# Weight tiles of sixteen blocks for eight, and more pairs of weight blocks by seven products, in a hybrid decoder layer

## The chip, the cores and the metric

The kernel runs on one core of a Trainium2 chip. The metric is device time in microseconds (us) of one execution. Before the change it is 1799.46 us, the median of three runs from 1799.2 to 1799.68.

## The reference, cut to what matters

One layer of a decoder for 264 tokens (a prompt of 256 and 8 sampled ones), width 2048, inner width of the feed-forward parts 5504. All inputs are float32.

```python
def swiglu(x, wg, wu, wd):
    return (jax.nn.silu(x @ wg) * (x @ wu)) @ wd
...
h = h + 0.5 * swiglu(rmsnorm(h, norm_ffn1), ffn1_gate, ffn1_up, ffn1_down)
mix, ... = mixing_block(rmsnorm(h, norm_mix), w_in, b_gates, conv_w, conv_b, norm_mlstm, norm_conv, w_out, ...)
h = h + mix
h = h + 0.5 * swiglu(rmsnorm(h, norm_ffn2), ffn2_gate, ffn2_up, ffn2_down)
y = rmsnorm(h, norm_final)
```

`mixing_block` is one projection `w_in`, four mLSTM heads beside a short gated convolution, and the projection `w_out`. The change touches how the weights of all these products are brought in and split, and how the products of the two feed-forward parts ("ffn 1", "ffn 2") are made.

## The kernel before

**Blocks and halves.** Activations lie with the width on the partitions: 16 blocks of 128 (`KB`) by 264 tokens. A weight block is 128 x 128. The inner width is 43 blocks, worked in two halves, 0 to 21 and 22 to 42. For each half comes first the gate and up products, one inner block after another (16 weight blocks each for gate and up, `product`, or `product_pair` for both at once), then the down products of that half, 16 output blocks of 22 or 21 weight blocks each, added to `h`. So the program is: ffn 1 with gate/up, down, gate/up, down; the mixing; ffn 2 in the same four stages; the last norm.

**Splitting.** TensorE multiplies in f16. A float32 weight tile `wraw` is split on the chip into a high half, written by ScalarE (`high`, L243), and a low half, written by VectorE from the raw weights and the high half (`low`, L251). Both lie in a tile `w`. A product takes three matmuls for each weight block: high by high, high by low, low by high (`three`, L325 to L327), each of 264 columns.

**Pairs by seven.** Two products over the same activations, gate and up of one inner block or two neighbouring output blocks of down, can be made together as a pair (`product_pair`). The main part, high by high, is ordinary (L390, 264 columns). The two small corrections of every four weight blocks (two of each product) are made with seven products of half the tokens, 132 columns, instead of eight (L374, L375). For that the kernel needs sums of the weight halves (`weight_sums`, four instructions on VectorE for each 2 x 8 weight blocks, L304, into a tile `s`), sums of the activations (`token_sums`, L362, called the forms, made once: for the gate/up products from the norm, for the down products from each eight finished inner blocks, by `act_form`), and afterwards a joining of the PSUM banks (`join`: a copy on ScalarE at L430, then L433 to L440 on VectorE). `GU_SEVEN` lists the inner blocks whose gate and up go by seven, 36 in all, every second one from block 7 of ffn 1, from block 3 of ffn 2, and from block 22 of both; `DOWN_SEVEN` lists 17 of the 32 pairs of output blocks by ffn and half.

**Tiles.** `weight_plan` lists all weight tiles in the order of use: tiles of up to eight blocks (`WK`), so two for a gate, two for an up, three for an output block of down; a pair's tiles alternate between its two rows. `fetch` (L264) takes the next of the plan: a DMA of the SP queue into one of six buffers `wraw`, the high half at once into one of seven buffers `w`, and the low half when `release` is called. With `lag` set the low half of a tile waits in `held` until the next `fetch`. `AHEAD` is how many tiles are on the way before one is used. The first two inner blocks, gate and up, are made together from sixteen small tiles of four weight blocks (`FIRST`, `products4`, L542), while the input and its norm come in.

**Order.** The order on each engine is that in which the program issues its instructions (`manual_schedule`). Work that follows a product is put off with `at(delta, ...)`: `tick` counts 1 at the start of a product and a half within it, and then runs what was put off to that count. So the joining of a pair and the decay of gate and up (`halves`) run one count behind the pair, and the splitting of an activation one count later.

**Another path.** The program also holds a path with float32 matmuls for inputs outside f16's range, taken after a check on the values; `half_size` tells the two apart, and the profiled execution is the f16 one.

## Time and profile before

| | |
|---|---|
| median of three runs | 1799.46 us |
| the profiled execution's own time | 1799.44 us |
| its span | 1797.7 us, granted clock of TensorE 0.998 |
| ScalarE, high halves (L243) | 692 instructions, 667.3 us |
| VectorE, low halves (L251, activations included) | 692 instructions, 800.6 us |
| VectorE, weight sums (L304) | 492 instructions in two groups, 164.6 and 155.8 us |
| DMA | 381.53 MB, mean 212 GB/s; the queue of the weights takes 61.2% of the 16 DMA engines |

The profile counts an engine as busy while an instruction of its kind runs; matmuls are pipelined, so their ends are modelled, and their spacing is read from their starts. In its rows `<-` stands for "written from", a bracket for the idle time before an instruction and what ended it, and a row of the waits reads: engine, what it was to write and its line, what it waited for, total us, times, longest. The stages in order of time: the start to 28 us, gate/up of ffn 1's first half to 239, its down to 353, gate/up of the second half to 572, down to 682; the mixing to 1104; ffn 2's stages to 1335, 1448, 1667 and 1778.

### The profile page before, as it was taken

Reading aid. Unit: us, or ns where it says so; the run is one execution under the profiler, and the core shown is the slowest. Engines: PE = TensorE matmul, PEld = TensorE weight load, DVE = VectorE, ACT = ScalarE, POOL = GpSimd, SP = SyncE. Lnnn points to the kernel's source line nnn. Section 1 sums busy time; section 2 is a strip of 40 time slices with the busy share of each in tenths; the row PEclk is TensorE's granted clock in tenths of the full one; section 3 lists DMA queues with packets and bytes.
Section 4 is the critical chain, followed back from the end, with each engine's and each line's share of the span. In section 5 each row is a group of like instructions: output and inputs, shape, how many; then the busy total and the mean of one; then the engine's idle time right before and its main releaser. Section 6 shows DMA issues by size and latency. Waiting matters only on the chain.

```text
span 1797.7 us, 45488 instructions
## 1 busy us (share of the span) xinstructions
PE 1780.6 (99%) x19080; PEld 1595.9 (89%) x19080; DVE 1565.6 (87%) x2528; ACT 901.8 (50%) x1571; POOL 145.4 (8%) x200
## 2 busy tenths in 40 slices
PE   9999999999999999999999999999999999999997
PEld 8899989999998988888888888899989999999896
DVE  8899979999998898788888866999988999999785
ACT  7544444444445445567566644444444344444443
POOL 0000000000000222222121032000000000000122
PEclk9999999999999999999999999999999999999999
DMA  9667666666666556888887655666666666666653
GB/s 301 205 203 219 190 214 194 198 205 211 202 199 192 184 175 218 291 300 274 282 276 243 223 189 173 204 206 209 197 208 193 205 197 220 200 202 200 192 184 111
DMA packets 118517, 381.53 MB, mean 212 GB/s; under 512 B 14972, under 2 KB 24796, under 8 KB 118304
## 3 DMA queue, kind: packets, MB, share of 16 engines
q1 hardware_dynamic: 109104, 350.53, 61.2%
q0 software_dynamic: 8256, 27.57, 4.5%
q8 instruction: 151, 2.47, 0.6%
q10 hardware_dynamic: 944, 0.45, 0.1%
q14 instruction: 62, 0.51, 0.1%
HBM read 366.72 MB, written 11.78 MB: 211 GB/s over the span
## 4 chain that ended last, share of the span: by engine, by line
PE 92%; DVE 5%; issue 1%; ACT 1%; DMA 0%; SPq 0%; DVEq 0%; ACTq 0%
PE ps L327 20%; PE ps L325 20%; PE ps L326 20%; PE ps L390 11%; PE ps L374 10%; PE ps L375 9%; DVE w L251 2%; DVE s L304 1%; PE ps L542 1%; PE ps L688 0%; PE ps L1393 0%; PE ps L1336 0%; PE ps L1291 0%; ACT w L243 0%; DMA wraw<-in_w1gu 0%
## 5 line engine op out<-in xcount | busy, mean ns | idle before, releaser
L251 DVE SCALAR_TENSOR_TENSOR w<-wraw,w 128x1024 f16<-128x1024 f32 (+3 forms) x692 | 800.6, 1181 | 77.4 <-ACT w L243 76.4
L243 ACT ACTIVATE w<-wraw 128x1024 f16<-128x1024 f32 (+3 forms) x692 | 667.3, 1007 | 169.9 <-issue 75.5
L325 PE MATMUL ps<-x,w 128*128 128x264 f16 x1536 | 423.9, 276 | 0.0
L326 PE MATMUL ps<-x,w 128*128 128x264 f16 x1536 | 423.9, 276 | 0.0
L327 PE MATMUL ps<-x,w 128*128 128x264 f16 x1536 | 423.9, 276 | 0.0
L327 PEld LDWEIGHTS <-w 128*128 128x128 f16 x3372 | 329.9, 98 | 50.1 <-DVE w L251 2.0
L326 PEld LDWEIGHTS <-w 128*128 128x128 f16 x3372 | 329.9, 98 | 49.4
L325 PEld LDWEIGHTS <-w 128*128 128x128 f16 x3372 | 330.2, 98 | 48.2 <-issue 0.6
L325 PE MATMUL ps<-xm,w 128*128 128x264 f16 x896 | 247.3, 276 | 0.0
L327 PE MATMUL ps<-xm,w 128*128 128x264 f16 x896 | 247.3, 276 | 0.0
L326 PE MATMUL ps<-xm,w 128*128 128x264 f16 x896 | 247.3, 276 | 0.0
L390 PEld LDWEIGHTS <-w 128*128 128x128 f16 x1886 | 181.4, 98 | 25.4
L375 PEld LDWEIGHTS <-s 128*128 128x128 f16 x1872 | 181.7, 97 | 0.0
L327 PE MATMUL ps<-a,w 128*128 128x264 f16 (+2 forms) x684 | 180.2, 269 | 1.1 <-DVE w L251 1.1
L374 PEld LDWEIGHTS <-s 128*128 128x128 f16 x1872 | 180.1, 96 | 0.6 <-DVE s L304 0.5
L325 PE MATMUL ps<-a,w 128*128 128x264 f16 (+2 forms) x684 | 180.2, 269 | 0.0
L326 PE MATMUL ps<-a,w 128*128 128x264 f16 (+2 forms) x684 | 180.2, 269 | 0.0
L304 DVE TENSOR_TENSOR s<-s,w 128x1024 f16<-128x1024 f16 (+2 forms) x246 | 164.6, 669 | 4.3
L304 DVE TENSOR_TENSOR s<-w 128x1024 f16<-128x1024 f16 (+2 forms) x246 | 155.8, 674 | 5.3
L390 PE MATMUL ps<-x,w 128*128 128x264 f16 x1152 | 141.3, 276 | 0.0
L375 PEld LDWEIGHTS <-w 128*128 128x128 f16 x1418 | 138.3, 98 | 2.9 <-DVE w L251 0.9
L374 PEld LDWEIGHTS <-w 128*128 128x128 f16 x1418 | 138.1, 97 | 2.0
(273 smaller groups left out, 2295.3 us busy)
## 6 DMA issues: line engine op xcount, KB each, us to landing
wraw<-in_w2gu SPq DMA_DIRECT2D x172, 512.0 KB, 4.6
wraw<-in_w1gu SPq DMA_DIRECT2D x164, 512.0 KB, 4.6
wraw<-in_win SPq DMA_DIRECT2D x112, 512.0 KB, 6.0
wraw<-in_w1d SPq DMA_DIRECT2D x42, 512.0 KB, 4.6
wraw<-in_w2d SPq DMA_DIRECT2D x38, 512.0 KB, 4.4
wraw<-in_w2d SPq DMA_DIRECT2D x42, 448.0 KB, 4.1
wraw<-in_wout SPq DMA_DIRECT2D x32, 512.0 KB, 4.5
wraw<-in_w1d SPq DMA_DIRECT2D x36, 448.0 KB, 4.1
```

Of the source, the lines that this page charges most:

```text
L243: nc.scalar.activation(dst, src, AF.Copy, scale=scale)
L251: nc.vector.scalar_tensor_tensor(dst, src, scale, hi, op0=ALU.mult, op1=ALU.subtract)
L304: nc.vector.tensor_tensor(s[:, out], x, y, op=ALU.add)
L325: nc.tensor.matmul(ps, wh, xk[:, 0, :], start=first, stop=False)
L326: nc.tensor.matmul(ps, wh, xk[:, 1, :], start=False, stop=False)
L327: nc.tensor.matmul(ps, wl, xk[:, 0, :], start=False, stop=last)
L374: nc.tensor.matmul(ps, w[0], x[:, 1], start=first, stop=False)
L375: nc.tensor.matmul(ps, w[1], x[:, 0], start=False, stop=last)
L390: nc.tensor.matmul(ps[:, :T], hi[:, i], xs[i][:, 0], start=(k0 + i == 0), stop=False)
L542: nc.tensor.matmul(ps[j0 + j], w[:, nk * j + k, :], x[k0 + k][:, part, :], start=(k0 + k + n == 0), stop=(k0 + k == KB - 1 and n == 2),)
```

## The change

Five things change together.

1. A weight tile holds sixteen blocks (`WIDE`) instead of eight. Gate, up and each block of the mixing projections are one tile each, an output block of down is two tiles (11 and 11 blocks, or 10 and 11). A pair's two rows lie in one tile, eight blocks of each, so that a gate/up pair is two tiles and a down pair three. There are three buffers of raw weights and four of halves, `AHEAD` is 3, and high and low halves alternate block by block within a tile. One transfer, one high and one low instruction serve a whole tile.
2. The four weight sums take three instructions: the first makes two of them, since b + d and c + d have the same second operand (L339 in the changed kernel), and the other two follow from them (L342, L343).
3. 44 instead of 36 inner blocks go by seven: of every five, the first, third and fourth. 19 instead of 17 output pairs, the two more in the first halves.
4. The small tiles of the start have rings of their own (`small`: eight raw, twelve split) in buffers that the sums and forms use later. The first two output blocks of the mixing are made from tiles that hold both (`products_two`), and the decays of the heads (`bc`) lie in the buffer of the joining.
5. `release` also runs at the start of a product and ahead of a pair's matmuls, and `fetch` in the middle of a product whose weights are one tile. Where two pairs are neighbours, the low half of the first one's activations comes one count earlier (`at(0.5, ...)`).

```diff
+WIDE = 16
...
-    n: [j for half in starts for j in half]
-    for n, starts in (
-        ("1", (range(7, 21, 2), range(22, NFB - 1, 2))), ("2", (range(3, 21, 2), range(22, NFB - 1, 2))),
-    )
+    n: [b0 + i for b0, b1 in ((first, 21), (22, NFB - 1)) for i in range(b1 - b0) if i % 5 in (0, 2, 3)]
+    for n, first in (("1", 7), ("2", 3))
 }
 DOWN_SEVEN = {
-    ("1", 0): (1, 3, 4, 6, 7), ("1", 1): (1, 3, 4, 6),
-    ("2", 0): (1, 3, 4, 6, 7), ("2", 1): (1, 3, 4),
+    ("1", 0): (1, 2, 3, 5, 6, 7), ("1", 1): (1, 3, 4, 6),
+    ("2", 0): (1, 2, 3, 5, 6, 7), ("2", 1): (1, 3, 4),
...
-        parts = -(-n // WK)
+        parts = -(-n // (WIDE if sevens else WK))
...
-    def beside(key, one, other, n):
+    def beside(key, rows, n):
+        rows = rows.rearrange("g p k m -> p g k m")
         for k0 in range(0, n, WK):
-            for w in (one, other):
-                plan.append((key, w[:, k0 : min(k0 + WK, n), :], min(WK, n - k0), 128, 1))
+            n_ = min(WK, n - k0)
+            plan.append((key, rows[:, :, k0 : k0 + n_, :], n_, 128, 2))
...
-                    beside((layer, "gu", j), gu[j, 0], gu[j, 1], KB)
+                    beside((layer, "gu", j), gu[j], KB)
...
-    for k0 in (0, half):
-        for db in range(2):
-            add(("out", db), a["wout"][db][:, k0 : k0 + half], half)
+    if sevens:
+        beside(("two", 0), a["wout"][0:2], KB)
+    else:
+        for k0 in (0, half):
+            for db in range(2):
+                add(("out", db), a["wout"][db][:, k0 : k0 + half], half)
...
-    AHEAD = 6 if half_size else 2
+    AHEAD = 3 if half_size else 2
...
-        raw = wpool.tile([128, WK, 128], F32, tag="wraw", name="wraw", bufs=AHEAD + (not half_size))[:, :n, :m]
-        dst = raw.rearrange("p (f k) m -> p f k m", f=several) if several > 1 else raw
-        nc.sync.dma_start(dst, src)
-        parts = wpool.tile([128, 2, WK, 128], PART, tag="w", name="w", bufs=AHEAD + 1)
-        hi, lo = parts[:, 0], parts[:, 1]
-        pairs = [(raw, (hi, lo), slice(0, m))]
-        if half_size and key == "gates":
-
-            pairs = [(raw[:, :, 32 * g :], (hi, lo), slice(16 * g, 16 * g + 16)) for g in (0, 1)]
+        if half_size and key == "four":
+            raw, parts = small()
+        elif half_size:
+            raw = wpool.tile([128, WIDE, 128], F32, tag="wraw", name="wraw", bufs=3)
+            parts = wpool.tile([128, WIDE, 2, 128], PART, tag="w", name="w", bufs=4)
+            raw = raw[:, :, :m]
...
+        elif several > 1:
+            raw, parts = raw[:, : several * n], parts[:, : several * n]
+            nc.sync.dma_start(raw.rearrange("p (g k) m -> p g k m", g=several), src)
+            pairs = [(raw, parts[:, :, 0], parts[:, :, 1])]
+        else:
+            raw, both = raw[:, :n], parts[:, :n]
+            nc.sync.dma_start(raw, src)
+            pairs = [(raw, both[:, :, 0, :m], both[:, :, 1, :m])]
...
-                beside.append(parts)
-                if len(beside) == 2:
-                    sums.append(weight_sums(*beside, tile_[3] // 2))
-                    beside.clear()
+                sums.append(weight_sums(parts, tile_[3]))
...
-    def weight_sums(one, other, n):
-
-        s = spool[0].tile([128, 4, 2, WK // 2, 128], PART, tag="s", name="s", bufs=3)[:, :, :, :n]
-        a_, b_, c_, d_ = (w[:, :, i : 2 * n : 2] for w in (one, other) for i in (0, 1))
-        for out, x, y in ((0, c_, d_), (1, b_, d_), (2, s[:, 0], b_), (3, s[:, 2], a_)):
-            nc.vector.tensor_tensor(s[:, out], x, y, op=ALU.add)
+    def small():
+        if not rings:
+            raws, parts = [], []
+            for g in range(2):
+                t = spool[0].tile([128, 16 * TH], F32, tag=f"g{g}", name=f"raw{g}")
+                t = t[:, :2048].rearrange("p (i k m) -> p i k m", i=4, k=4)
+                raws += [t[:, i] for i in range(4)]
+            for g in range(3):
+                t = spool[0].tile([128, 4, 4, 2, 128], PART, tag="s", name="part", bufs=3)
+                parts += [t[:, i] for i in range(4)]
+            rings.extend((raws, parts))
+        for r in rings:
+            r.append(r.pop(0))
+        return [r[-1] for r in rings]
+    def weight_sums(w, n):
+        m = n // 2
+        s = spool[0].tile([128, 4, WK // 2, 2, 128], PART, tag="s", name="s", bufs=3)[:, :, :m]
+        a_, b_, d_ = (w[:, i : i + 2 * m - 1 : 2] for i in (0, 1, n + 1))
+        bc = w[:, 1 : 2 * n - 1].rearrange("p (g k) h m -> p g k h m", g=2)[:, :, 0 : 2 * m - 1 : 2]
+        nc.vector.tensor_tensor(
+            s[:, 0:2], bc, d_.unsqueeze(1).to_broadcast([128, 2, m, 2, 128]), op=ALU.add
+        )
+        nc.vector.tensor_tensor(s[:, 2], s[:, 1], b_, op=ALU.add)
+        nc.vector.tensor_tensor(s[:, 3], s[:, 2], a_, op=ALU.add)
...
-    def product(key, x, order, m=128, lead=AHEAD):
+    def product(key, x, order, m=128, soon=False):
         tick()
+        if lag[0]:
+            release()
         ps = bank()[:m, :T]
-        k, half = 0, 0.5
-        while k < len(order):
-            while plan and len(ready) + len(held) < lead:
+        count, k, half = len(order), 0, 0.5
+        while k < count:
+            while plan and len(ready) + len(held) < AHEAD:
                 fetch()
             got, hi, lo, n = ready.pop(0)
             assert got == key, (got, key)
+            one = half_size and n == count
+            if soon and k == 0:
+                fetch()
             for i in range(n):
                 three(
-                    ps, hi[:, i, :m], lo[:, i, :m], x[order[k]], k == 0, k == len(order) - 1
+                    ps, hi[:, i, :m], lo[:, i, :m], x[order[k]], k == 0, k == count - 1
                 )
                 k += 1
-            if lead == AHEAD and (k < len(order) or lag[0]):
+                if one and i == n // 2 - 1 and not soon:
+                    fetch()
+                if one and i == n // 2 - 1:
+                    tick(half)
+            if not one and not soon and (k < count or lag[0]):
                 fetch()
-            tick(half)
-            half = 0
+            if not one:
+                tick(half)
+                half = 0
...
-            tiles = []
-            for _ in range(2):
-                while plan and len(ready) + len(held) < AHEAD or not ready:
-                    fetch()
-                tiles.append(ready.pop(0))
-                assert tiles[-1][0] == key, (tiles[-1][0], key)
-            (_, hi0, lo0, n), (_, hi1, lo1, _) = tiles
+            while plan and len(ready) + len(held) < AHEAD or not ready:
+                fetch()
+            got, hi, lo, n = ready.pop(0)
+            assert got == key, (got, key)
+            release()
             s = sums.pop(0)
+            (hi0, lo0), (hi1, lo1) = ((hi[:, r:], lo[:, r:]) for r in (0, n))
...
-            if k0 < count:
-                fetch()
...
-                    if len(ready) > 2 and more:
+                    if more:
...
-                    at(1.5, low, *rest)
+                    at(0.5 if j in sevens and j + 1 in sevens else 1.5, low, *rest)
...
-                            lead=AHEAD - 3 if final else AHEAD,
+                            soon=final,
...
-            self.bc = mp.tile([128, 2, SEQ], F32, tag="bc", name="bc", bufs=1)
+            if e["half_size"]:
+                bc = tmp.tile([128, 5 * TH], F32, tag="y5", name="bc", bufs=1)
+                self.bc = bc[:, : 2 * SEQ].rearrange("p (j t) -> p j t", j=2)
+            else:
+                self.bc = mp.tile([128, 2, SEQ], F32, tag="bc", name="bc", bufs=1)
```

How this stands on VectorE is shown at three places. The rows are in the order of the program; names carry buffer numbers, L-numbers are those of each kernel. The changed kernel's lines L254, L339 to L343, L411, L479 and L895 are before's L251, L304, L362, L433 and L827.

First, the second half of ffn 1's gate/up, behind the joining of a pair. Before, this is block 24; `w_5872` and `w_5893` are the first two of the four tiles of pair 26, and the ordinary block 25 lies between:

```order
L827 TENSOR_TENSOR y5_5952<-y5_5952,rstd_668 128x528
L251 SCALAR_TENSOR_TENSOR w_5893<-wraw_5891,w_5893 128x1024
L304 TENSOR_TENSOR s_5993<-w_5893 128x1024
L304 TENSOR_TENSOR s_5993<-w_5872,w_5893 128x1024
L304 TENSOR_TENSOR s_5993<-s_5993,w_5872 128x1024 x2
L251 SCALAR_TENSOR_TENSOR w_5990<-wraw_5988,w_5990 128x1024
L846 TENSOR_TENSOR ta_6027<-ps_5963,rstd_668 128x264
```

In the changed kernel this is the joining of block 29, whose neighbour 30 is a pair too; `w_6463` and `w_6554` are the gate and the up tile of the ordinary block 31 behind them:

```order
L895 TENSOR_TENSOR y5_6522<-y5_6522,rstd_621 128x528
L254 SCALAR_TENSOR_TENSOR w_6463<-wraw_6462,w_6463 128x16x128
L863 TENSOR_TENSOR y5_6522<-y5_6522,tb_6524 128x264
L254 SCALAR_TENSOR_TENSOR w_6554<-wraw_6553,w_6554 128x16x128
L254 SCALAR_TENSOR_TENSOR a0_5510<-y5_6522,a0_5510 128x264
L479 TENSOR_TENSOR y5_6693<-y5_6693,ps_6535 128x132
```

Before, the tile behind a joining was the second of the four tiles of a pair that comes after another block; now it is the whole gate tile of the block that comes behind the next pair, and the next joining follows two such tiles.

Second, the forms of the activations. Before (`w_6775` is the last up tile of block 31, `w_6838` the first tile of pair 32):

```order
L251 SCALAR_TENSOR_TENSOR a0_5711<-y5_6596,a0_5711 128x264
L251 SCALAR_TENSOR_TENSOR a0_5711<-tc_6743,a0_5711 128x264
L251 SCALAR_TENSOR_TENSOR w_6775<-wraw_6773,w_6775 128x1024
L362 TENSOR_TENSOR g0_6841<-a0_5711 128x1056 x2
L362 TENSOR_TENSOR g0_6841<-g0_6841,a0_5711 128x1056
L362 TENSOR_TENSOR g0_6841<-a0_5711,g0_6841 128x1056
L251 SCALAR_TENSOR_TENSOR w_6838<-wraw_6836,w_6838 128x1024
L433 TENSOR_TENSOR y5_6923<-y5_6923,ps_6751 128x132
```

In the changed kernel, between the joinings of blocks 37 and 39 (`w_7945` is the second tile of pair 40):

```order
L254 SCALAR_TENSOR_TENSOR a1_6774<-y5_7778,a1_6774 128x264
L254 SCALAR_TENSOR_TENSOR a2_7916<-tc_7913,a2_7916 128x264
L411 TENSOR_TENSOR g1_8006<-a1_6774 128x1056 x2
L411 TENSOR_TENSOR g1_8006<-g1_8006,a1_6774 128x1056
L411 TENSOR_TENSOR g1_8006<-a1_6774,g1_8006 128x1056
L254 SCALAR_TENSOR_TENSOR w_7945<-wraw_7944,w_7945 128x16x128
L339 TENSOR_TENSOR s_8012<-w_7945 128x2048
L342 TENSOR_TENSOR s_8012<-s_8012,w_7945 128x1024
L343 TENSOR_TENSOR s_8012<-s_8012,w_7945 128x1024
L479 TENSOR_TENSOR y5_8092<-y5_8092,ps_7922 128x132
```

The forms are the same four instructions; behind them stood one low half of eight blocks ahead of the next joining, and now stand a whole pair tile's low half and sums.

Third, the end of the first product, where the first ordinary tiles follow the small ones. Before (`w_464` and `w_481` are the last small tiles, `w_498` and `w_503` the first two of the next gate):

```order
L251 SCALAR_TENSOR_TENSOR x11_340<-h12_83,gains_165,x11_340 128x264 x2
L251 SCALAR_TENSOR_TENSOR w_464<-wraw_462,w_464 128x512
L251 SCALAR_TENSOR_TENSOR w_481<-wraw_479,w_481 128x512
L251 SCALAR_TENSOR_TENSOR w_498<-wraw_496,w_498 128x1024
L251 SCALAR_TENSOR_TENSOR w_503<-wraw_501,w_503 128x1024
L752 TENSOR_TENSOR sq0_506<-sq0_506 128x528
```

In the changed kernel (`w_470` and `w_479` are the next gate and up):

```order
L254 SCALAR_TENSOR_TENSOR x11_329<-h12_83,gains_165,x11_329 128x264 x2
L254 SCALAR_TENSOR_TENSOR part_198<-raw1_197,part_198 128x4x128 x2
L254 SCALAR_TENSOR_TENSOR w_470<-wraw_469,w_470 128x16x128
L820 TENSOR_TENSOR sq0_474<-sq0_474 128x528
L254 SCALAR_TENSOR_TENSOR w_479<-wraw_478,w_479 128x16x128
L820 TENSOR_TENSOR sq0_474<-sq0_474 128x528 x2
```

The low half of the first ordinary tile covers sixteen blocks in one instruction where two of eight stood, and the first of the norm's squares (L820) now stands ahead of the up tile.

More of the change, by code (lines that the diff above doesn't have):

```diff
@@ L119, in ffn @@
             for db in range(0, KB, 2):
-                one, other = (d[i][:, b0:b1, :] for i in (db, db + 1))
+                both = d[db : db + 2][:, :, b0:b1, :]
                 if sevens and db // 2 in DOWN_SEVEN[layer, half]:
-                    beside((layer, "dd", half, db), one, other, b1 - b0)
+                    beside((layer, "dd", half, db), both, b1 - b0)
                 else:
-                    add((layer, "d", half, db), one, b1 - b0)
-                    add((layer, "d", half, db + 1), other, b1 - b0)
+                    for i in range(2):
+                        add((layer, "d", half, db + i), both[i], b1 - b0)
     four = a["w1gu"][0:2].rearrange("j g p k m -> p (j g) k m")
@@ L277, in fetch @@
         release()
-        held.append((lows, (key, hi, lo, n), parts))
+        held.append((lows, (key, parts[:, :, 0], parts[:, :, 1], n), parts))
         if not lag[0]:
@@ L290, in release @@
             if tile_[0][1] in ("gu", "dd"):
[L291 to L294 removed]
+                sums.append(weight_sums(parts, tile_[3]))
         held.clear()
[L297 to L304 removed]
+    sums, spool, rings = [], [None], []
+    def small():
[22 more added lines that the diff above has]
+        nc.vector.tensor_tensor(s[:, 3], s[:, 2], a_, op=ALU.add)
         return s
@@ L404, in product_pair @@
                     a_, b_, c_ = (hi0[:, e], lo0[:, e]), (hi0[:, o], lo0[:, o]), (hi1[:, e], lo1[:, e])
-                    w = (a_, b_, c_, *((s[:, f, 0, i], s[:, f, 1, i]) for f in range(4)))[f]
+                    w = (a_, b_, c_, *((s[:, f, i, 0], s[:, f, i, 1]) for f in (1, 0, 2, 3)))[f]
                     ps, rhs, own = (
@@ L450, in product_beside, with products_two @@
         ps = bank()[:, :T]
+        while plan and len(ready) + len(held) < AHEAD:
+            fetch()
+        got, hi, lo, n = ready.pop(0)
+        assert got == key and n == KB, (got, key, n)
+        for k in range(0, n, 4):
+            for term, (w, part) in enumerate(((hi, 0), (hi, 1), (lo, 0))):
+                for c in range(4):
+                    nc.tensor.matmul(
+                        ps[32 * c : 32 * c + 32], w[:, k + c, :32],
+                        x[k + c][:, part, :], start=(k + term == 0),
+                        stop=(k + 4 == KB and term == 2), tile_position=(0, 32 * c),
+                    )
+            if k == KB // 2 - 4:
+                fetch()
+        return ps
+    def products_two(x, order):
+        ps = [bank()[:, :T] for _ in range(2)]
         for k0 in range(0, KB, WK):
+            tick()
             while plan and len(ready) + len(held) < AHEAD:
@@ L454, in product_beside @@
             got, hi, lo, n = ready.pop(0)
-            assert got == key and n == WK, (got, key, n)
-            for k in range(0, n, 4):
-                for term, (w, part) in enumerate(((hi, 0), (hi, 1), (lo, 0))):
-                    for c in range(4):
-                        nc.tensor.matmul(
-                            ps[32 * c : 32 * c + 32], w[:, k + c, :32],
-                            x[k0 + k + c][:, part, :], start=(k0 + k + term == 0),
-                            stop=(k0 + k + 4 == KB and term == 2), tile_position=(0, 32 * c),
-                        )
-            if k0 + n < KB:
-                fetch()
+            assert got == ("two", 0) and n == WK, got
+            for j in range(2):
+                for i in range(n):
+                    k = k0 + i
+                    three(
+                        ps[j], hi[:, WK * j + i], lo[:, WK * j + i], x[order[k]], k == 0,
+                        k == KB - 1,
+                    )
+                if j == 0:
+                    fetch()
+                    tick(0.5)
         return ps
     def products2(keys, x, order):
+        if half_size:
+            return products_two(x, order)
         ps = [bank()[:, :T] for _ in keys]
```

19 lines of the change are left out of this document (15 added, 4 removed).

## The prediction

> **What bounds the kernel now.** I read the page first, then what TensorE (PE) waited for, then both engines in order of time.
>
> ```profile
> PE 1780.6 (99%) x19080; PEld 1595.9 (89%) x19080; DVE 1565.6 (87%) x2528; ACT 901.8 (50%) x1571; POOL 145.4 (8%) x200
> ```
> ```profile
> PE ps L1019 <- DVE ok L1013: 2.3, 1, 2.3
> PE ps L542 <- ACT w L243: 1.3, 2, 0.8
> ```
> PE is the bound: its two longest waits of the whole span are a 2.3 us one in the last microseconds and 1.3 us in the first product. A busy share alone would not prove that the matmuls are dense, so the spacing is read from the order of time:
>
> ```profile
> 82.75 1.96 PE L390 MATMUL ps<-x,w 128*128 128x264 f16 x16
> ...
> 92.79 0.28 PE L325 MATMUL ps<-x,w 128*128 128x264 f16 x1
> ...
> 103.59 0.61 PE L390 MATMUL ps<-x,w 128*128 128x264 f16 x4
> ```
> A gate/up block done by seven ("P") takes 92.79 - 82.75 = 10.04 us, an ordinary block ("N") 103.59 - 92.79 = 10.80 us. So what fewer matmuls save is real time, if their weights are ready.
>
> VectorE (DVE), which makes the low halves and the sums, is nearly full where P and N alternate. Its waits in 353 to 572 us (a second half of gate/up, 219 us) are all of these:
>
> ```profile
> DVE w L251 <- ACT w L243: 6.0, 11, 1.5
> DVE y L433 <- ACT y L430: 2.5, 3, 1.0
> DVE ta L846 <- PE ps L327: 1.6, 1, 1.6
> DVE a L251 <- ACT a L243: 1.1, 2, 0.6
> DVE tc L852 <- PE ps L327: 0.7, 1, 0.7
> ```
> 11.9 us of 219: DVE is occupied 94.6% at one pair in two blocks. The question is whether it can carry three in five.
>
> **The change part by part.**
>
> *Fewer matmul columns.* Eight more gate/up pairs (36 to 44) at 10.80 - 10.04 = 0.76 us: 6.1 us. Two more down pairs (17 to 19), both in first halves. Such a pair lasts 353.23 - 339.42 = 13.81 us:
>
> ```profile
> 339.42 1.96 PE L390 MATMUL ps<-a,w 128*128 128x264 f16 x16
> ...
> 353.23 0.95 PE L390 MATMUL ps<-x,w 128*128 128x264 f16 x7
> ```
> Two ordinary products of 22 blocks are 132 matmuls at 10.80/96 = 0.1125 us, 14.85 us; two pairs save 2.1 us. **PE saves 8.2 us.**
>
> *What DVE pays for a tile.* One period of before, from the joining of a pair's banks (L433) to the next:
>
> ```profile
> 426.33 0.29 DVE L433 TENSOR_TENSOR y<-y,ps 128x132 f32<-128x132 f32 x1 [0.98 <-ACT y L430]
> ...
> 428.98 1.22 DVE L251 SCALAR_TENSOR_TENSOR w<-wraw,w 128x1024 f16<-128x1024 f32 x1
> 430.24 1.29 DVE L304 TENSOR_TENSOR s<-w 128x1024 f16<-128x1024 f16 x2
> 431.45 1.41 DVE L304 TENSOR_TENSOR s<-s,w 128x1024 f16<-128x1024 f16 x2
> 432.78 1.22 DVE L251 SCALAR_TENSOR_TENSOR w<-wraw,w 128x1024 f16<-128x1024 f32 x1
> 433.91 0.43 DVE L846 TENSOR_TENSOR ta<-ps,rstd 128x264 f32<-128x264 f32 x1
> ...
> 442.01 1.22 DVE L251 SCALAR_TENSOR_TENSOR w<-wraw,w 128x1024 f16<-128x1024 f32 x1 [0.46 <-ACT w L243]
> ...
> 444.98 1.32 DVE L362 TENSOR_TENSOR g<-a 128x1056 f16<-128x1056 f16 x2
> ...
> 447.58 1.22 DVE L251 SCALAR_TENSOR_TENSOR w<-wraw,w 128x1024 f16<-128x1024 f32 x1
> 448.72 0.28 DVE L433 TENSOR_TENSOR y<-y,ps 128x132 f32<-128x132 f32 x1
> ```
> Joining: 428.98 - 426.33 = 2.65 us. A low half costs 1.13 (432.78 to 433.91), or 1.26 when the next instruction reads its result (428.98 to 430.24); four sums 2.54 (430.24 to 432.78). So a pair's 16 blocks cost 1.13 + 1.26 + 2.54 = 4.93 us. The forms of the activations (L362) take 2.60 us, once in eight blocks. Without them and the 0.46 wait the period is 448.72 - 426.33 - 0.46 - 2.60 = 19.33; less joining, two pair tiles (9.86) and the four lows of N (4.6) it leaves 2.2 for N's evacuations and the splits of activations.
>
> ```profile
> L251 DVE SCALAR_TENSOR_TENSOR w<-wraw,w 128x1024 f16<-128x1024 f32 x560 | 675.4, 1229 | 65.0 <-ACT w L243 64.4
> ...
> L251 DVE SCALAR_TENSOR_TENSOR w<-wraw,w 128x512 f16<-128x512 f32 x16 | 11.1, 692 | 3.3 <-ACT w L243 2.9
> ```
> From 692 ns for 512 elements and 1229 for 1024 comes 1.05 ns an element; 2048 elements are about 2.2 us, 2.3 with a reader behind. So joining two instructions saves only some 0.07 to 0.15 us. The wide sum of 2048 at 0.53 ns an element (0.605 each in the first two sums) is 1.14, the other two 1.33, and the second of the three now reads what the one just ahead wrote: 2.47 to 2.6. **A wide pair tile costs DVE T = 4.73 (no bubble) to 5.00 us (no gain at all, and slightly worse); I take 4.85**, nearest to the rows with their readers; a wide tile of N 2.2.
>
> [...]
>
> One more row of before, the joining of the last of two neighbouring down pairs, whose 353.23 stands above:
>
> ```profile
> 358.24 0.29 DVE L433 TENSOR_TENSOR y<-y,ps 128x132 f32<-128x132 f32 x1
> ```
>
> *How late DVE gets.* In the new order, stretches run P N P P N. Between joinings, against PE:
> - pair, N, pair, followed by another pair (four pair tiles queued): 2.65 + 4 x 4.85 + 2.2 = 24.25 against 20.84: 3.4 later.
> - the two neighbours: 2.65 + two N tiles 4.4 + 0.7 = 7.75 against 10.04: 2.3 caught up.
> - from there over N to the single pair: 2.65 + 9.7 + 4.4 + 2.2 = 18.95 against 20.84: 1.9 caught up.
> - forms: 2.6 later.
>
> A cycle of five costs DVE 50.95 + 2.6 x 5/8 = 52.6 us, PE only 51.7. It no longer fits; the reserve decides. The tightest tile is the gate tile of the N behind two neighbours: its low stands behind the joining of the first neighbour, and PE wants it one pair (10.04 us, plus two matmuls 0.23) after that joining may start. Joining 2.65, low 2.2 and ScalarE's copy ahead of them 0.35 leave 5.1 us. So 3.4 fits, 3.4 + 2.6 does not: PE stands about 0.9 us where the forms fall between. Carried along joining by joining from the order (lateness below zero is lost): ffn 1 first half 0.9 at block 11 and 1.0 at 21; second half 0.6 at 26 (three down pairs in a row and block 22 arrive 7 us late; before, the latest there was 358.24 - 353.23 = 5.0), 1.0 at 36, 1.8 at 41; ffn 2 first half 0.1, since its forms fall beside single pairs; second half again 3.4. **About 8.8 us of new PE waits**; 1.4 with T = 4.73, 22 with T = 5.00.
>
> Three down pairs in a row lose 2.3 us each on DVE, but the next N's lows come 5 us ahead of need: nothing there.
>
> *The start.* The first ordinary tile is now 1 MB. Before:
>
> ```profile
> 20.44 1.08 SPq L264 DMA_DIRECT2D wraw<-in_w1gu  x2
> ```
> ```profile
> 25.39 1.06 ACT L243 ACTIVATE w<-wraw 128x1024 f16<-128x1024 f32 x1 [0.65 <-PE ps L542]
> 26.80 1.06 ACT L243 ACTIVATE w<-wraw 128x1024 f16<-128x1024 f32 x1 [0.35 <-DMA wraw<-in_w1gu]
> ```
> ```profile
> 28.08 0.28 PE L327 MATMUL ps<-x,w 128*128 128x264 f16 x1
> ```
> The second half-megabyte landed just ahead of 26.80. Converted as one tile, high 1.9 and low 2.3 us end at 31.0, and PE's third matmul wants the low at 28.08: 2.9 us lost. Against that, the small tiles of the start get a ring of their own, eight deep, and the first three wide transfers wait for no buffer (the row at 20.44 is SP, held up to there by six); the data may land 2 us sooner, which leaves 0.9. I take **1.3 us**, bounds 0 to 2.9, for the freed queue acts from the first tiles on.
>
> *Edits at nothing.* Half as many, larger DMAs: the same bytes, three buffers of 1 MB for six of half; a buffer is refilled within three tiles of 5 us. ScalarE's highs are joined at 50% load. The decays in the buffer of the joining, the order of the first two output products, and the last products hide under PE work of 5 us a tile; 2 us if that cover fails. The second-half down pairs are unchanged.
>
> *Sum:* -8.2 + 8.8 + 1.3 = +1.9 us on the profiled execution's 1799.44 us (span 1797.7; the median of the runs, 1799.46, is the same): **1801.3 us**.
>
> **The rivals.**
> 1. *The reserve holds.* T near 4.73 or below: 1.4 us of waits, start 0.5: 1799.4 - 8.2 + 1.9 = 1793. For it: the fewer instructions. Against it: the bubbles in the rows at 428.98 and 431.45.
> 2. *Lateness adds up* (slower). If a wide tile costs DVE 5.00, as the eight-block ones do where two lows precede their sums, waits reach 22 us: 1799.4 - 8.2 + 22 + 1.3 = 1814.5. The place is the N behind two neighbours, all four gate/up halves; it turns slower than before at T of about 4.83, and past the bound below at 4.88.
> 3. *The joined sum loses its rate* (slower): its second operand is one half-tile read twice. At one element for two, the wide sum takes 2.2 us, T is 5.9, and 145 pair tiles would cost over 100 us. The trace has no f16 sum with such an operand. [...]
>
> **How the numbers follow.** What a measurement of this kernel can tell from no change is about 0.2%, 3.6 us: 1795.9 to 1803.1. The forecast, waits of 4 to 13 us, 1797 to 1805.5: 0.40, of which 0.28 lie within the bound and 0.12 above. Rival 1: 0.39, of which 0.03 within. Rival 2: 0.18. Rival 3: 0.03. Faster 0.36, same 0.31, slower 0.33. Both signs hold much of the chance, so the range reaches from 1791 (rival 1 with a free start) to 1811; beyond it lie rival 3 and the far half of rival 2.
>
> **What would show it.** Right: PE waits of about a microsecond each for the low (now L254) at blocks 11, 21, 26, 36, 41, one of 1 to 3 us near 28 us, DVE without idle time between, pair blocks still 10.04 us. Rival 1: DVE waits for ScalarE in every cycle and PE waits for nothing. Rival 2: waits at every second N. Wrong altogether: pair blocks longer than 10.04 us, or PE waiting for a DMA.

## The result, and the profile after

The changed kernel takes 1855.8 us (median of 4 runs, 1855.56 to 1855.82) against 1799.45: a ratio of 1.0313, with a 95% interval of 1.0295 to 1.0331. Slower by 56 us, where 1801.3 was forecast and 1811 was the end of the range. The profiled execution took 1855.79 us, its span is 1854.1, the granted clock 0.990.

The page's busy times, then what TensorE (PE) waited for (total us, times, longest):

```profile
PE 1790.9 (97%) x19596; PEld 1600.9 (86%) x19596; DVE 1617.1 (87%) x2196; ACT 864.8 (47%) x1216; POOL 160.1 (9%) x200
...
DVE 47%; PE 39%; issue 6%; ACT 4%; DMA 4%; POOL 1%; SPq 0%; DVEq 0%; ACTq 0%; POOLq 0%
```
```profile
PE ps L366 <- DVE w L254: 34.1, 21, 4.0
PE ps L424 <- DVE w L254: 7.5, 8, 1.6
PE ps L1228 <- DVE gl L1217: 2.4, 1, 2.4
...
PE ps L756 <- ACT sq L1564: 2.1, 2, 1.4
...
PE ps L504 <- ACT xm L246: 1.0, 1, 1.0
```
Before, the chain and PE's waits for low halves were these:

```profile
PE 92%; DVE 5%; issue 1%; ACT 1%; DMA 0%; SPq 0%; DVEq 0%; ACTq 0%
```
```profile
PE ps L327 <- DVE w L251: 1.1, 3, 0.4
...
PE ps L375 <- DVE w L251: 0.6, 1, 0.6
```
The line of shares is the chain of work that ended last, followed back from the last instruction: it ran 92% through PE before, now 47% through VectorE (DVE). The bound has moved. VectorE's busy share has not (87% before and after); a share of the span can't show this. The low halves that PE hardly waited for (1.1 and 0.6 us before) now stop it 29 times for 41.6 us.

The worst of these waits, on both engines in order of time. Pair 24 ends where the first row begins pair 25, and the ordinary block 26 follows; VectorE joins pair 24 at L479:

```profile
395.21 1.96 PE L438 MATMUL ps<-x,w 128*128 128x264 f16 x16
...
400.56 2.28 DVE L254 SCALAR_TENSOR_TENSOR w<-wraw,w 128x2048 f16<-128x2048 f32 x1
402.94 1.23 DVE L339 TENSOR_TENSOR s<-w 128x2048 f16<-128x2048 f16 x1
404.20 0.69 DVE L342 TENSOR_TENSOR s<-s,w 128x1024 f16<-128x1024 f16 x1
404.93 0.69 DVE L343 TENSOR_TENSOR s<-s,w 128x1024 f16<-128x1024 f16 x1
405.54 0.28 DVE L479 TENSOR_TENSOR y<-y,ps 128x132 f32<-128x132 f32 x1
...
408.18 2.28 DVE L254 SCALAR_TENSOR_TENSOR w<-wraw,w 128x2048 f16<-128x2048 f32 x1
...
406.26 0.28 PE L365 MATMUL ps<-x,w 128*128 128x264 f16 x1
410.52 0.29 PE L366 MATMUL ps<-x,w 128*128 128x264 f16 x1 [3.99 <-DVE w L254]
```
No idle time stands between VectorE's rows here. Pair 24 is done at 395.2, and its joining begins at 405.54; the low half of block 26 stands behind it and ends after 410, and PE's third matmul needs it. The tile ahead took 405.54 - 400.56 = 4.98 us.

A little earlier VectorE, though late, did stand idle. ScalarE waits 9.47 us for the joining of pair 22, the next high half stands behind that, and VectorE waits for the high half:

```profile
386.90 0.42 ACT L898 ACTIVATE tb<-y 128x264 f32<-128x264 f32 x1 [9.47 <-DVE y L895]
...
389.15 2.29 DVE L254 SCALAR_TENSOR_TENSOR w<-wraw,w 128x2048 f16<-128x2048 f32 x1 [1.37 <-ACT w L246]
```
So lateness on VectorE comes back to it by way of ScalarE. The same 1.37 us stands at 1518.04, ahead of PE's other long wait (3.98 us, block 26 of ffn 2).

What follows that wait, with other stretches of the same kind (us, busy times of the engines with instructions, then granted clock, DMA share, GB/s):

```profile
410.00:420.00 10.00, 9.48 (x70) 7.54 (x71) 9.40 (x14) 5.29 (x6) 0.00 (x0) 0.83 0.67 221
...
660.00:670.00 10.00, 6.11 (x61) 4.59 (x58) 9.83 (x14) 3.61 (x5) 4.45 (x4) 0.88 0.31 82
670.00:680.00 10.00, 10.00 (x86) 8.54 (x85) 8.20 (x13) 5.97 (x8) 5.33 (x6) 0.95 0.93 331
...
1530.00:1540.00 10.00, 5.62 (x73) 4.71 (x72) 9.69 (x14) 2.49 (x3) 0.00 (x0) 0.90 0.36 118
1540.00:1550.00 10.00, 10.00 (x70) 7.81 (x68) 9.37 (x13) 4.44 (x5) 0.00 (x0) 0.76 0.73 244
```
The stretches 230 to 240, 570 to 580, 740 to 750 and 1700 to 1710 show 0.83 too. Within all these the clock is 0.50, seen by the microsecond, for about 3.4 us at a time:

```profile
413.00:414.00 1.00, 1.00 (x7) 0.66 (x5) 0.61 (x3) 0.34 (x2) 0.00 (x0) 0.50 1.01 406
```
PE is "busy" all the while, but this row holds 7 matmuls, parts of some included, where 8.9 fit into a microsecond. The missing clock adds up to 13.6 us (each 0.83 is 1.7 us of ten). Before, no such stretch lay within the work (clock 1.00 up to 1790 us).

**Where 56.4 us of span come from.** Fewer matmul columns: -8.2. More waiting for low halves: 41.6 - 1.7 = 39.9. A wait's row counts from the modelled end of the matmul before (0.28 us), though the next would have started after 0.11: 29 x 0.17 = 5. Half clock: 13.6. Three waits in the mixing (L1228, L756, L504; the first 0.7 us before, the others nothing): 4.8. Sum 55.1; 1.3 us stay unassigned. (About 1.2 us of the half clock lies inside waits, where no matmul runs, and is counted twice, so the unassigned rest is nearer 2.5.)

### The profile page after: what moved, and what is told of

It reads as the page before. It is cut to its first block, busy times and chain, and to the rows that moved or that the text cites. A ratio compares the mean times of both kernels' runs of the same rounds, so it can differ in the third digit from the quotient of the medians.

```text
span 1854.1 us, 44580 instructions
## 1 busy us (share of the span) xinstructions
PE 1790.9 (97%) x19596; PEld 1600.9 (86%) x19596; DVE 1617.1 (87%) x2196; ACT 864.8 (47%) x1216; POOL 160.1 (9%) x200
## 3 DMA queue, kind: packets, MB, share of 16 engines
q8 instruction: 155, 2.54, 0.6%
## 4 chain that ended last, share of the span: by engine, by line
DVE 47%; PE 39%; issue 6%; ACT 4%; DMA 4%; POOL 1%; SPq 0%; DVEq 0%; ACTq 0%; POOLq 0%
DVE w L254 20%; PE ps L366 11%; PE ps L364 11%; PE ps L365 11%; DVE s L339 8%; DVE s L342 4%; ACT w L246 2%; DVE s L343 2%; PE ps L438 2%; PE ps L424 2%; PE ps L423 2%; DMA wraw<-in_w1d 1%; DVE y L895 1%; DVE y L480 1%; DVE a L254 1%
## 5 line engine op out<-in xcount | busy, mean ns | idle before, releaser
L254 DVE SCALAR_TENSOR_TENSOR w<-wraw,w 128x2048 f16<-128x2048 f32 (+3 forms) x351 | 753.5, 2151 | 86.3 <-ACT w L246 86.1
L246 ACT ACTIVATE w<-wraw 128x2048 f16<-128x2048 f32 (+3 forms) x351 | 620.1, 1780 | 197.2 <-DMA wraw<-in_w1d 66.3
L366 PE MATMUL ps<-x,w 128*128 128x264 f16 x1280 | 358.0, 280 | 28.5 <-DVE w L254 28.4
L364 PE MATMUL ps<-x,w 128*128 128x264 f16 x1280 | 357.8, 280 | 0.0
L365 PE MATMUL ps<-x,w 128*128 128x264 f16 x1280 | 357.6, 279 | 0.0
L424 PEld LDWEIGHTS <-s 128*128 128x128 f16 x2216 | 215.1, 97 | 0.0
L423 PEld LDWEIGHTS <-s 128*128 128x128 f16 x2216 | 213.1, 96 | 1.8 <-DVE s L343 1.1
L339 DVE TENSOR_TENSOR s<-w 128x2048 f16<-128x2048 f16 (+2 forms) x145 | 173.1, 1194 | 7.7
L438 PE MATMUL ps<-x,w 128*128 128x264 f16 x1408 | 172.8, 276 | 0.0
L366 PE MATMUL ps<-a,w 128*128 128x264 f16 (+2 forms) x596 | 156.8, 270 | 5.7 <-DVE w L254 5.7
L364 PE MATMUL ps<-a,w 128*128 128x264 f16 (+2 forms) x596 | 156.7, 270 | 0.0
L365 PE MATMUL ps<-a,w 128*128 128x264 f16 (+2 forms) x596 | 156.7, 269 | 0.0
L423 PE MATMUL ps<-f,s 128*128 128x132 f16 x1056 | 130.8, 220 | 0.0
```

The lines of the kernel that those rows point to most:

```text
L246: nc.scalar.activation(dst, src, AF.Copy, scale=scale)
L254: nc.vector.scalar_tensor_tensor(dst, src, scale, hi, op0=ALU.mult, op1=ALU.subtract)
L339: nc.vector.tensor_tensor(s[:, 0:2], bc, d_.unsqueeze(1).to_broadcast([128, 2, m, 2, 128]), op=ALU.add)
L364: nc.tensor.matmul(ps, wh, xk[:, 0, :], start=first, stop=False)
L365: nc.tensor.matmul(ps, wh, xk[:, 1, :], start=False, stop=False)
L366: nc.tensor.matmul(ps, wl, xk[:, 0, :], start=False, stop=last)
```

## The experiments

Two theories were set against each other at first. A: VectorE has more work than fits. B: the wide tiles leave too short a lead, so that a late low half reaches PE at once. Times are medians against before's 1799.4 to 1799.6 of the same series.

**The parts of the change apart.** The changed kernel with the lists of pairs of before:

```diff
-    n: [b0 + i for b0, b1 in ((first, 21), (22, NFB - 1)) for i in range(b1 - b0) if i % 5 in (0, 2, 3)]
+    n: [j for half in starts for j in half]
...
-    ("1", 0): (1, 2, 3, 5, 6, 7), ("1", 1): (1, 3, 4, 6),
+    ("1", 0): (1, 3, 4, 6, 7), ("1", 1): (1, 3, 4, 6),
...
```


> The changed kernel with the 36 and 17 pairs of before: wide tiles, three buffers and sums in three instructions alone. Theory A (VectorE has more work than fits, because of the added pairs: a wide pair tile costs it 4.95 us and a stretch of five blocks 53.2 us against PE's 51.7): 1799 to 1806 us, PE waits for low halves under 6 us, nearly all of it the 1.9 us at the start. Theory B (the wide tiles take the lead away: a late low half frees its raw buffer late, so the next transfer and high half are late too): 1820 to 1850 us, with PE waits still 1 to 3 us each in gate/up.

Measured: 1815.7 us (ratio 1.0087, 1.007 to 1.0104). Neither: below B, above A. Its waits of PE:

```profile
PE ps L368 <- DVE w L256: 7.1, 7, 2.1
...
PE ps L426 <- DVE w L256: 1.7, 2, 1.3
```
The gate/up stages of ffn 1 are nearly free of waits again, those of ffn 2 but for one of 1.69 us; what is left stands at the start (1.07 us), in the second halves of down (5.6 us) and in the mixing.

The kernel of before with the new lists, and the earlier low half between neighbours:

```diff
-                    at(1.5, low, *rest)
+                    at(0.5 if j in sevens and j + 1 in sevens else 1.5, low, *rest)
```


> The kernel of before with the 44 and 19 pairs of the change (and the earlier low half of the activations where two pairs are neighbours, which the single joining buffer needs): the pairs alone. Theory A: VectorE's work per pair tile is the same 4.93 us in the narrow form, so it is as slow as the change, 1835 to 1860 us, with PE waits of 2 to 4 us and half-clock stretches after the longest. Theory B: the six smaller buffers give the lead back, 1792 to 1806 us.

Measured: 1829.5 us (1.0166, 1.015 to 1.0183), again between the two. So the pairs alone cost 30 us, the rest of the change (the wide tiles with their buffers, the joined sum, the new order) 16, both 56: more than their sum.

The changed kernel with only the down pairs of before:

> The changed kernel with the 17 down pairs of before and the 44 gate/up pairs: two pairs fewer cost PE 2.1 us. Theory A: the waits in the first halves of down (6.2 us) and much of the 4.0 us wait at block 26 of both parts, with its half clock (1.7 and 3.4 us), go: 1838 to 1847 us. Theory B: the gate/up waits stay, 1847 to 1855 us.

Measured: 1841.7 us, 14 us faster than the change though PE has 2.1 us more to do: as A foretold. Part of it is the clock. The profile of this run (its fastest execution, 1838.1 us) has 6.8 us of half clock for 13.6: waits of 2.85, 2.67 and 2.66 us, about as long as the change's at the same blocks, have none here.

**VectorE's work.** The changed kernel without the last of the three sums (the seventh product takes the third sum in its place, so it leaves a part of the corrections out):

```diff
-        nc.vector.tensor_tensor(s[:, 3], s[:, 2], a_, op=ALU.add)
...
-                    w = (a_, b_, c_, *((s[:, f, i, 0], s[:, f, i, 1]) for f in (1, 0, 2, 3)))[f]
+                    w = (a_, b_, c_, *((s[:, f, i, 0], s[:, f, i, 1]) for f in (1, 0, 2, 2)))[f]
```


> The changed kernel without the last of the three weight sums; the seventh product takes the third sum in its place, so its weights are not the reference's. A pair tile then costs VectorE about 4.25 us for 4.9, and a stretch of five blocks 49.3 us against PE's 51.7. Theory A (VectorE's amount of work): the waits in gate/up (27 us) and their half-clock stretches go nearly all, and what is left over the saved 8.2 us is what the wide tiles alone showed (16 us): 1800 to 1810 us. Theory B (too short a lead, whatever the work): half or more of the gate/up waits stay, 1825 to 1850 us.

Measured: 1799.4 us. Some 0.69 us less for each of 145 pair tiles, 100 us of VectorE, is worth 56 us. In its profile PE waits for low halves at the start (1.76 us) and once near the end (0.42), and nowhere else. The waits in the second halves of down are gone too. The 8.2 us saved are lost to what is left of the other edits, at the start and in the mixing, 3.4 us of it to half clock behind a wait of 2.12 us there. The time is just under A's range and far from B's: VectorE's work is the cause.

The three sums against four, in the wide tile:

```diff
-        nc.vector.tensor_tensor(
-            s[:, 0:2], bc, d_.unsqueeze(1).to_broadcast([128, 2, m, 2, 128]), op=ALU.add
-        )
-        nc.vector.tensor_tensor(s[:, 2], s[:, 1], b_, op=ALU.add)
-        nc.vector.tensor_tensor(s[:, 3], s[:, 2], a_, op=ALU.add)
+        for out, x, y in ((1, c_, d_), (0, b_, d_), (2, s[:, 1], b_), (3, s[:, 2], a_)):
+            nc.vector.tensor_tensor(s[:, out], x, y, op=ALU.add)
```


> The changed kernel with the weight sums in four instructions again (each half of the joined one by itself, in the order of before). In the changed kernel's profile the three sums took 418.72 to 421.31 = 2.59 us, in before's the four 2.54. Theory: the joined sum saves nothing, since the two that follow each wait for the one just ahead: 1846 to 1857 us. Rival: one instruction fewer does save VectorE time that counts: 1859 to 1875 us.

Measured: 1846.7 us, 9 us faster than the change. In the order of time, the change's low half and sums first, then the four sums of this run, each up to their follower:

```profile
416.40 2.29 DVE L254 SCALAR_TENSOR_TENSOR w<-wraw,w 128x2048 f16<-128x2048 f32 x1
418.72 1.23 DVE L339 TENSOR_TENSOR s<-w 128x2048 f16<-128x2048 f16 x1
419.98 0.69 DVE L342 TENSOR_TENSOR s<-s,w 128x1024 f16<-128x1024 f16 x1
420.70 0.69 DVE L343 TENSOR_TENSOR s<-s,w 128x1024 f16<-128x1024 f16 x1
421.31 0.42 DVE L914 TENSOR_TENSOR ta<-ps,rstd 128x264 f32<-128x264 f32 x1
```
```profile
416.99 1.29 DVE L340 TENSOR_TENSOR s<-w 128x1024 f16<-128x1024 f16 x2
418.20 1.41 DVE L340 TENSOR_TENSOR s<-s,w 128x1024 f16<-128x1024 f16 x2
419.53 0.42 DVE L911 TENSOR_TENSOR ta<-ps,rstd 128x264 f32<-128x264 f32 x1
```
2.59 us (418.72 to 421.31) against 2.54: with one instruction fewer the sums take longer, since L342 now follows directly on L339, whose result it reads. L339 takes 1.26 us up to it, the two separate sums 1.21 (416.99 to 418.20); the two sums behind them take 1.33 in both kernels. What a reader behind costs shows in L342 too, 0.72 us up to L343, which reads it, where L343 with an independent follower takes 0.61. 0.05 us in 145 tiles is 7 us of VectorE, and the time moved by 9.

Work taken off VectorE another way, the product of up and decayed gate on GpSimd:

```diff
-                nc.vector.tensor_tensor(zu, zu, sg, op=ALU.mult)
+                side.tensor_tensor(zu, zu, sg, op=ALU.mult)
```


> The changed kernel with the product of up by the decayed gate (one instruction of 264 columns for each block, 0.35 us of VectorE) on GpSimd, which is 9% busy. That takes 1.75 us of 53.2 from VectorE in a stretch of five blocks, which then just fits PE's 51.7. Theory A: half or more of the gate/up waits go, 1815 to 1840 us. Theory B: no more than 5 us better than the change, 1850 to 1856 us. If GpSimd slows VectorE where both run, slower than the change.

> Tiles of eight blocks with the 44 and 19 pairs, and the same product on GpSimd: 1829.5 us without that. Theory A: the waits of some 18 us in gate/up mostly go, 1803 to 1815 us. Theory B (lead): they were there with the longer lead too, so nothing is foretold by it; a gain under 5 us would speak against A. If GpSimd slows VectorE, above 1829 us.

Measured: 1873.1 and 1847.6 us, 17 and 18 us slower than without. The groups of the first, and of the change (count, busy us, mean ns):

```profile
L863 POOL TENSOR_TENSOR y<-y,tb 128x264 f32<-128x264 f32 x44 | 89.7, 2040 | 653.3 <-ACT tb L898 653.3
L339 DVE TENSOR_TENSOR s<-w 128x2048 f16<-128x2048 f16 x126 | 172.0, 1365 | 7.4 <-DVE w L254 0.5
```
```profile
L863 DVE TENSOR_TENSOR y<-y,tb 128x264 f32<-128x264 f32 x44 | 18.7, 425 | 0.4 <-ACT tb L898 0.4
L339 DVE TENSOR_TENSOR s<-w 128x2048 f16<-128x2048 f16 x126 | 155.4, 1233 | 7.0
```
What VectorE does in 425 ns takes GpSimd 2040, and the joined sum on VectorE rises from 1233 to 1365 ns: VectorE gained 0.35 us a block and lost part of it, the third case of the expectations. In the second run the same products took GpSimd 1041 and 1378 ns (its spans are rough), and VectorE's first sums rose from 688 to 755 ns. The activations come later besides, by some 1.6 us a block in the first run (2040 - 425 ns). As a test of A these two say little.

**The lead.** Before, with one tile of eight less on the way, then the same with the new pairs:

```diff
-    AHEAD = 6 if half_size else 2
+    AHEAD = 5 if half_size else 2
```


> The kernel of before with one tile of eight blocks less on the way: five raw buffers for six, six of halves for seven. VectorE's work is the same. Theory A: within 2 us of before, since VectorE fits at one pair in two blocks. Theory B: PE waits of 0.5 to 2 us for low halves in gate/up and down, 1803 to 1820 us.

> Tiles of eight blocks, the 44 and 19 pairs, and one tile less on the way (five raw buffers, six of halves). The pairs alone cost 30.0 us and one tile less of lead 11.7 us. If the two only add: 1841 us. If a shorter lead makes each late stretch of an overfull VectorE reach PE (theory: work and lead decide together): 1845 to 1865 us, near the change. If the width of a tile by itself is what the change lost beside the pairs: under 1838 us.

Measured: 1811.2 us (+11.7) and 1875.0 us (+45.6 over the new pairs with the full lead, beyond the 1845 to 1865 us foretold). What PE waits for in the second:

```profile
PE ps L325 <- DVE w L249: 44.5, 28, 2.9
PE ps L388 <- ACT w L241: 7.1, 8, 1.1
```
So B holds as well, and the two are one mechanism: overwork makes VectorE late, the lead says how much of that PE sees. The same tile less costs 12 us where VectorE fits and 46 where it does not; in its profile some 20 us are half clock, of which the run with the full lead has none before its end.

**The road by which it reaches PE.** The held low half ahead of the joining, so that no N tile stands behind it:

```diff
+        release()
         tick()
         one, other, more = bank(), bank(), bank()
```


> The changed kernel with the held low half released ahead of the joining of the pair before, at the start of a pair. If the place of the low half (behind the joining) is what costs, the waits at the ordinary blocks behind two neighbours go: 1815 to 1835 us. If VectorE's amount of work is what costs (theory A), the lateness only moves to another tile or to the joining: 1845 to 1858 us.

Measured: 1881.1 us, 25 us slower than the change; worse than either view. ScalarE, then VectorE, at the same place:

```profile
417.21 0.42 ACT L899 ACTIVATE tb<-y 128x264 f32<-128x264 f32 x1 [9.88 <-DVE y L896]
...
419.47 2.29 DVE L254 SCALAR_TENSOR_TENSOR w<-wraw,w 128x2048 f16<-128x2048 f32 x1 [1.37 <-ACT w L246]
```
The decay of the gate (L899) waits 9.88 us on ScalarE for the later joining, the next high half stands behind it, and VectorE, the engine without time, waits 1.37 us for that. In the feed-forward parts of the change this wait stands twice (389.15 and 1518.04), in those of this run 15 times; PE's waits for low halves grow from 41.6 to 64.6 us.

Then the matmuls of an ordinary tile in another order, all of the high half first:

```diff
             for i in range(n):
-                three(
-                    ps, hi[:, i, :m], lo[:, i, :m], x[order[k]], k == 0, k == count - 1
-                )
+                for part in range(2):
+                    nc.tensor.matmul(
+                        ps, hi[:, i, :m], x[order[k]][:, part, :], start=(k + part == 0), stop=False
+                    )
                 k += 1
...
+            for i in range(n):
+                nc.tensor.matmul(
+                    ps, lo[:, i, :m], x[order[k - n + i]][:, 0, :], start=False,
+                    stop=(k == count and i == n - 1),
+                )
```


> The changed kernel with the matmuls of an ordinary tile in another order: both products of the high half for all its blocks first, then those of the low half. The same matmuls; the low half of a tile of sixteen is wanted 32 x 0.1125 - 0.23 = 3.4 us later, of a down tile of eleven 2.2 us later. If the early need of the low half is the road by which a late VectorE stops TensorE: the waits at ordinary blocks (34 us) and the half-clock stretches behind the longest mostly go, 1810 to 1825 us. If the lateness reaches the pairs anyway: 1845 to 1855 us.

> Tiles of eight blocks with the 44 and 19 pairs and the same order of matmuls; the low half is wanted 16 x 0.1125 - 0.23 = 1.6 us later. Without it 1829.5 us, with 17.8 us of waits at ordinary blocks, most of them 0.3 to 0.9 us. Early need: 1808 to 1818 us. Lateness reaches the pairs: 1824 to 1829 us.

> Wide tiles, four separate sums, and the low-half matmuls last. Early need: 9 us or somewhat less below the run with the joined sum, 1803 to 1818 us. Lateness reaches the pairs: 1836 to 1846 us.

Measured: 1841.3, 1826.6 and 1834.1 us: 14.5, 2.9 and 12.6 us gained. In the wide tiles that is a little better than "the lateness reaches the pairs anyway", in the narrow ones as it says, and in all far from "early need". The waits of the first:

```profile
PE ps L430 <- DVE w L254: 22.5, 20, 2.2
...
PE ps L394 <- DVE w L254: 3.7, 7, 0.6
```
The low halves of ordinary tiles (L394) are hardly waited for any more. The lateness passes them and arrives at the corrections of the pairs (L430). The waits are shorter than the change's, 26.2 us for 41.6, and the half clock of this profile is 6.8 us for 13.6.

**A version that beats both.** Tiles of eight, 40 gate/up pairs and the 17 down pairs of before; one neighbour in each half, where VectorE comes rested or can recover:

```diff
-        ("1", (range(7, 21, 2), range(22, NFB - 1, 2))), ("2", (range(3, 21, 2), range(22, NFB - 1, 2))),
+        ("1", ([7, *range(8, 21, 2)], [*range(22, NFB - 2, 2), 41])),
+        ("2", ([3, *range(4, 21, 2)], [*range(22, NFB - 2, 2), 41])),
```


> The kernel of before with one more gate/up pair in each half (40 for 36; the added neighbour at the start of the first halves, 7 and 8 or 3 and 4, and at the end of the second, 40 and 41), and the earlier low half of the activations there. PE saves 4 x 0.76 = 3.0 us. VectorE pays 5.7 us more in each half, where it has some 8 us to spare. If that reserve covers it: 1796 to 1798 us. If the neighbours make a tile late: 1800 to 1808 us.

Measured: 1796.6 us (11 runs, 1796.4 to 1797.07), ratio 0.9984, interval 0.9975 to 0.9993. PE's waits for low halves are what they were before the change:

```profile
PE ps L328 <- DVE w L252: 1.1, 3, 0.4
...
PE ps L376 <- DVE w L252: 0.6, 1, 0.6
```
2.8 us gained of 3.0 worked out (0.16%; the slowest of the 11 runs is faster than the fastest of before's 15): as long as nothing is late, saved columns are saved time.

## Why the prediction was wrong, point by point

The forecast missed the time by 54.5 us. By the traces some 18 of them are waits in gate/up, 12 waits in down, 13.6 half clock, 5 what a wait costs beyond its row, 4.8 the mixing. The first was in the sum and mis-sized; the waits in down and in the mixing were put at nothing; the half clock and what a wait costs beyond its row were not in it.

- **Columns: right.** The first pair of the changed kernel takes 94.85 - 84.80 = 10.05 us,

```profile
84.80 1.97 PE L438 MATMUL ps<-x,w 128*128 128x264 f16 x16
...
94.85 0.28 PE L364 MATMUL ps<-x,w 128*128 128x264 f16 x1
```
and the run with 40 pairs returned 0.7 us for each pair added.
- **The price of a tile: too low.** T = 4.85 was taken; the rows show 4.91 (416.40 to 421.31) to 4.98 us. The step that failed is the choice "nearest to the rows with their readers" between 4.73 and 5.00: one instruction fewer was credited with a gain, though the text itself named the new reader behind the joined sum. The run with four sums shows the gain to be a loss of 9 us. Its parts, 2.3 us for a low half with a reader and 2.47 to 2.6 for the sums, add up to 4.77 to 4.9, not to 4.73 to 5.00; they measured 2.32 and 2.59, the upper end.
- **The place: right.** The waits fall where the joining was foreseen ahead of the gate tile: blocks 11, 21, 26, 36 and 41. The sizes were off: 1.45, 2.84, 3.99, 1.30 and 2.84 us for the forecast 0.9, 1.0, 0.6, 1.0 and 1.8 in ffn 1; and 1.80 and 1.19 us in ffn 2's first half, where 0.1 was forecast. A wait of 1.31 us at block 23 of both parts was not foreseen. All gate/up waits add up to 27 us for 8.8.
- **Down: wrong.** "Nothing there" failed: VectorE is busy for 39.72 of 41 us where the first three down pairs are,

```profile
266.00:307.00 41.00, 39.17 (x548) 36.59 (x546) 39.72 (x48) 15.37 (x14) 0.00 (x0) 1.00 0.51 166
```
```profile
280.41 0.28 DVE L479 TENSOR_TENSOR y<-y,ps 128x132 f32<-128x132 f32 x1
...
296.74 0.77 DVE L675 TENSOR_REDUCE downs<-ps 128x1 f32<-128x264 f32 x2
297.42 0.28 DVE L479 TENSOR_TENSOR y<-y,ps 128x132 f32<-128x132 f32 x1
```
and joins two neighbours 297.42 - 280.41 = 17.0 us apart where 13.8 + 2.3 = 16.1 was reckoned and PE takes 13.8. Only 0.3 of these 0.9 us are the same T (two tiles of sixteen blocks); 0.68 is the reduction L675 ahead of the joining, which the forecast does not name. That gives waits of 6.2 us in the first halves of down, and hands more lateness to the gate/up half behind them: the joining of block 24 begins 10.3 us after the pair's end, where the forecast had 5.7 (5.1 of reserve and a wait of 0.6) and a copy of 0.35. The wait of VectorE for ScalarE, 1.37 us at 389.15, is part of that; "ScalarE's highs at 50% load" looked at the load and not at the order of its queue. The run with the old down pairs returned 14 us. The second halves of down, put at nothing because their pairs did not change, wait for 5.9 us; with the pairs of before they still do (5.6), with one sum less they do not (0.4).
- **The half clock: a term that was missing.** Waits were counted once; the seven longest within the work came with slow matmuls, 13.6 us.
- **The start:** 1.9 us for 1.3, within its bounds. **Edits at nothing:** the mixing lost 4.8 us and one of the half-clock stretches. No wait of PE in the list is for a DMA, but the chain holds 4% of transfers (0% before), some of which start only when a late low half has freed their buffer (two low halves end at 306.93, the transfer starts at 306.96); VectorE then idles for the high half behind the transfer:

```profile
306.96 6.60 DMA wraw<-in_w1d
```
```profile
315.61 2.29 DVE L254 SCALAR_TENSOR_TENSOR w<-wraw,w 128x2048 f16<-128x2048 f32 x1 [2.13 <-ACT w L246]
```
The forecast's "refilled within three tiles" left this out.
- **A small reading:** the "1.3 us in the first product" before the change are two waits, the longer 0.8 us.
- **The rivals.** "Lateness adds up" was the right one, at a chance of 0.18, with its sign, place and condition (T of 4.88 and more). Its 22 us of waits were near the 27 measured in gate/up; its time, 1814.5, fell short by the two terms above that no case held, down and the clock, and by the mixing. "The joined sum loses its rate" did not happen: 1233 ns for 2048 elements is less than two sums of 688 before. What was lost lay between the instructions: 2.59 us from the first row to the follower, against 2.54 for the four sums.

Not settled: how much of the 16 us without the new pairs is the lump (the low half of sixteen blocks arrives at once), how much the fewer, larger buffers and how much the joined sum. Its waits in down are VectorE's work as well, since they go with one sum less. A fourth raw buffer of sixteen blocks was not tried.

## What to carry to other kernels

Where an engine off the path is 95% occupied in a stage, each instruction given to it must be priced with its follower (0.72 us for a sum that the next one reads, 0.61 for one that it does not), and the sum must fit the bound engine's time over every stretch, not the mean; here the step past that point cost 56 us where it could gain 8. The lead of the buffers decided here how much lateness was forgiven (one tile less cost 12 us where VectorE fits, 46 where it does not), and the change, which adds work and coarsens the lead at once, lost more than both apart (56 us for 30 and 16). Add such work in small steps, where a rested stretch lies ahead of it, and stop at the first wait.

## What the runs showed of the hardware

- TensorE's granted clock fell to 0.50 for 3.41 us (234.09 to 237.50 us in the changed kernel), once for twice that (1537.98 to 1544.80), at some of its waits. In the changed kernel waits of 2.07 (with one of 1.59 us ahead of it), 2.42, 2.67, 2.84, 3.98 and 3.99 us had it, one of 1.93 us did not. The length of a wait alone does not decide: in the run with the old down pairs this one and another of 2.67 us (to 565.28) had none:

```profile
234.60 0.29 PE L366 MATMUL ps<-x,w 128*128 128x264 f16 x1 [2.85 <-DVE w L254]
```
In the changed kernel the slow stretches begin at 234.09, 411.58, 572.00, 667.58, 742.67, 1537.98 and 1701.82 us, which are 52, 47, 28, 22, 233 and 48 times 3.413 us apart (the first distance, 177.49 us, divided by 52). So these seven starts lie on one beat, five of them before the wait has ended (234.09 in a wait that ends at 234.26). In the run with the old down pairs, reckoned from its slow stretch at 404.07, the beat falls at 233.40 and 564.50, within the two waits that had none; but in the changed kernel it falls at 408.17, 667.58 and 1537.98 within waits that had one (3.99, 2.07 and 3.98 us). What decides between them is not shown.
- GpSimd needed 2040 ns in one run and 1041 in another for a float32 product of 128 x 264 that VectorE makes in 425, and VectorE's sums beside it took 10 to 11% longer (755 ns for 688, 1365 for 1233).
